# Rotary embedding and scores on one Trainium2 core: the first piece of q is issued on ScalarE's DMA queue instead of SyncE's

## The chip and the metric

The kernel runs on one core of one Trainium2 chip. The metric is the device time of one execution in microseconds. Engines are named as in the profile: PE is TensorE, PEld its weight loads, DVE is VectorE, ACT ScalarE, POOL GpSimd, SP SyncE.

## The reference

Queries and keys of 16 batches, 512 positions, 16 heads and 64 channels are rotated by the tables cos and sin, and then every query position of a head is multiplied with every key position of the same head. All is in float32.

```python
# q, k: (16, 512, 16, 64); cos, sin: (512, 32); q1, q2 (k1, k2) are the halves of the 64 channels
q_rot = concat([q1 * cos - q2 * sin, q1 * sin + q2 * cos])
k_rot = concat([k1 * cos - k2 * sin, k1 * sin + k2 * cos])
scores = einsum('bshd,bthd->bsht', q_rot, k_rot)      # (16, 512, 16, 512)
```

The inputs are 67 MB, the output is 268 MB.

## The kernel before

A batch is 512 positions. Partition p holds the positions 4p to 4p+3 (`C` = 4), so a batch of q or k is one tile of 128 partitions by 4 x 1024 numbers, 2 MB, loaded by one DMA (`load`, L122, on SyncE's queue). Five of these later loads go through GpSimd's queue instead (`load_around`, L84 and L98).

The work goes in 64 steps `i`, four for each batch; a step makes the scores of one of the four position groups, 128 positions by 16 heads by 512 keys, 4 MB. For a step, VectorE rotates (`rope`: products at L149 and L150, the sum at L154), TensorE transposes the rotated tiles into PSUM banks (L170), ScalarE or VectorE copies these to `qT_t` and `kT_t` (L185), TensorE multiplies (`scores`, L201), ScalarE copies the products to the staging tile `st` (L208), and SyncE issues the store: for the first batch one 1 MB store for each quarter of the heads (L211), later one 4 MB store for each step (L188). There are three staging buffers. The whole order is written out by hand (`tc.manual_schedule()`): on each engine instructions run in the order of the program, and a DMA is issued when its engine comes to it.

The first batch is treated otherwise, so that work can begin before 4 MB have come. Its q and k go into one tile, `early`, in pieces by heads: first four heads of k (`G` = 4 heads, 512 KB, 128 partitions x 4 runs of 1 KB), then four heads of q, then the other twelve heads of k (1.5 MB, runs of 3 KB), then those of q, each one DMA of `load_units` (L67). The two small tables `cos_t` and `sin_t` (64 KB each) are loaded on ScalarE's queue (L225). After its two loads ScalarE loads its function table, waits for `sin_t`, and makes `ss_t`, the sine with both signs (L232, L233). VectorE begins with the four heads of k, goes on with the four heads of q, and then, in the loop over `i` = 0 to 3, with the other head groups of the first batch and the first tiles of the second.

The order of the first issues on SyncE is: k four heads, q four heads, k twelve heads, q twelve heads, k of batch 1, q of batch 1 (L67 four times, L122 twice); next on SyncE come the stores of step 0.

Of the kernel before, what the change touches and what calls it, by code (L numbers as in the profile page):

```python
# [10 lines left out]
def kernel(  # L11
# [8 lines left out]
    nc = tc.nc  # L20
# [4 lines left out]
    B, S, H, D = q.shape  # L25
# [5 lines left out]
    G = H // C  # L31
# [27 lines left out]
    units = {}  # L59
    used = [0]  # L60

    def load_units(which, head, heads):
        n = C * heads * D
        t = early[:, used[0] : used[0] + n].rearrange("p (c e) -> p c e", c=C)
        used[0] += n
        src = dram[which][0, :, :, head : head + heads, :]
        nc.sync.dma_start(t.rearrange("p c (h d) -> p c h d", d=D), src)  # L67
        for h in range(0, heads, G):
            units[which, (head + h) // G] = t[:, :, D * h : D * (h + G)]

# [42 lines left out]
    def load(which, b):  # L113

        if b >= B:
            return
        t = in_pool.tile([P, C, H * D], fp32, tag=which + "_in", name=which + "_sb")
        batches[which, b] = t
        if (which, b) in RELIEVED:
            load_around(which, b, t)  # L120
        else:
            nc.sync.dma_start(t.rearrange("p c (h d) -> p c h d", h=H), dram[which][b])  # L122

    def rope(which, n):


        part = part_pool.tile([P, H * D], fp32, tag="part", name="part")
        if n < C:
            x = units[which, n]
            sv, k1, k2 = "p c (g j) -> p c g j", {"j": HD}, {"j": D}  # L130
            cs = cos_t.unsqueeze(2).to_broadcast((P, C, 2 * G, HD))
            ss = ss_v.unsqueeze(2).to_broadcast((P, C, G, D))
            pv = part.rearrange("p (c g j) -> p c g j", c=C, j=D)
            x5 = x.rearrange("p c (h x j) -> p c h x j", x=2, j=HD)
            p5 = part.rearrange("p (c h x j) -> p c h x j", c=C, x=2, j=HD)
            adds = [(x5[:, :, :, y], p5[:, :, :, 1 - y]) for y in range(2)]
        else:
            x = batches[which, n // C][:, n % C]
            sv, k1, k2 = "p (g j) -> p g j", {"j": HD}, {"j": D}
            cs = cos_t[:, n % C].unsqueeze(1).to_broadcast((P, 2 * H, HD))  # L140
            ss = ss_v[:, n % C].unsqueeze(1).to_broadcast((P, H, D))
            pv = part.rearrange(sv, **k2)
            x4 = x.rearrange("p (h x j) -> p h x j", x=2, j=HD)
            swapped = bass.AP(part.tensor, part.offset + HD, [part.ap[0], (D, H), (-HD, 2), (1, HD)])
            adds = [(x4, swapped)]
        xs, xc = x.rearrange(sv, **k2), x.rearrange(sv, **k1)

        def products():
            nc.vector.tensor_tensor(pv, xs, ss, op=mult)  # L149
            nc.vector.tensor_tensor(xc, xc, cs, op=mult)  # L150

        def sums():
            for y, z in adds:
                nc.vector.tensor_tensor(y, y, z, op=add)  # L154

        return [products, sums]
# [33 lines left out]
    def scores(i, p, st):  # L190

        ps = ps_s_pool.tile([P, 2, S], fp32, tag="ps_s", name="ps")
        b = i // C
        if b == 0:
            c, hp = divmod(p, 2)
            lhs, rhs = qT[i][:, C * hp + c], kT[0][:, 2 * i + hp]
        else:
            lhs, rhs = qT[i][:, p], kT[b][:, p]
        for r in range(2):
            po, rh = ps[:, r, :], rhs[64 * r : 64 * r + 64, :]  # L200
            nc.tensor.matmul(  # L201
                out=po, lhsT=lhs[64 * r : 64 * r + 64, :], rhs=rh, start=True, stop=True
            )
        so, si = st[:, 2 * p : 2 * p + 2, :], ps
        if b > 0:
            so = so.rearrange("s r (t c) -> s r t c", c=C)
            si = si.rearrange("s r (c t) -> s r t c", c=C)
        nc.scalar.copy(out=so, in_=si)  # L208
        if b == 0 and p % 2 == 1:
            c = p // 2  # L210
            nc.sync.dma_start(o_v[0, c, :, G * i : G * (i + 1)], st[:, G * c : G * (c + 1)])  # L211
        elif b > 0 and p == HP - 1:
            store(i, st)

    def tr_act(which, n):
        for g in range(2):
            transposed(which, n, g, nc.scalar.copy)

    def run(ops):
        for op in ops:  # L220
            op()

    with tc.manual_schedule():
        for t, src in ((cos_t, cos), (sin_t, sin)):
            nc.scalar.dma_start(t, src.rearrange("(p c) j -> p c j", c=C))  # L225
        for head, heads in ((0, G), (G, H - G)):
            load_units("k", head, heads)
            load_units("q", head, heads)
        load("k", 1)
        load("q", 1)  # L230
        make_identity(nc, ident)
        nc.scalar.copy(out=ss_t[:, :, 0, :], in_=sin_t)  # L232
        nc.scalar.mul(ss_t[:, :, 1, :], sin_t, -1.0)  # L233
        for which in ("k", "q"):
            run(rope(which, 0))
            tr_act(which, 0)


        for i in range(C):
            st = st_first[i] if i < 2 else stage_pool.tile([P, H, S], fp32, tag="stage", name="st")  # L240
            if i < C - 1:
                dve = rope("k", i + 1) + rope("q", i + 1) + rope("k", C + i)
                nxt = [("k", i + 1), ("q", i + 1)]
            else:
                dve = rope("q", C) + rope("k", C + i) + rope("q", C + 1) + rope("k", 2 * C)
                nxt = [("q", C), ("k", C + i)]
            for p in range(HP):
                scores(i, p, st)
                if p in (0, 1) and i > 0:
                    run(dve[:1])  # L250
                    dve = dve[1:]
                    transposed("k", C + i - 1, p, nc.vector.tensor_copy)
                if p == 3 and i < 2:
                    load("kq"[i], 2)
                if p in (2, 6):
                    m = len(dve) - (4 if p == 2 else 2) - (2 if i == C - 1 else 0)
                    run(dve[:m])
                    dve = dve[m:]
                    tr_act(*nxt.pop(0))
            run(dve)  # L260
        load("k", 3)


        for i in range(C, NST):
            tr = {}
            if i + 1 < NST:
                tr[1], tr[3] = ("q", i + 1, 0), ("q", i + 1, 1)
            if i + C < NST:
                tr[5], tr[6] = ("k", i + C, 0), ("k", i + C, 1)
            dve = []  # L270
            if i + 2 < NST:
                dve += rope("q", i + 2)
            if i + 1 + C < NST:
                dve += rope("k", i + 1 + C)
            st = stage_pool.tile([P, H, S], fp32, tag="stage", name="st")
            for p in range(HP):
                scores(i, p, st)
                if p not in tr:
                    continue
                if tr[p][0] == "q":  # L280
                    run(dve[:1])
                    dve = dve[1:]
                    transposed(*tr[p], nc.vector.tensor_copy)
                else:
                    transposed(*tr[p], nc.scalar.copy)
            run(dve)
            if i % C == C - 2:
                load("q", i // C + 2)
            elif i % C == C - 1:
                load("k", i // C + 3)  # L290
# [30 lines left out]
```

## Time and profile before

| what | value |
|---|---|
| runs | 793.13, 792.9, 793.66 us; median 793.13 us |
| span of the profiled execution, first to last instruction | 790.4 us |
| median of the runs less that span | 2.7 us |
| PE, ACT, DVE busy | 684.4, 562.0, 544.7 us |
| DMA | 336.18 MB, mean 425 GB/s over the span |
| first issue, first VectorE product, first store issued | 0.74, 5.67, 19.52 us |
| granted TensorE clock, mean | 0.934 |

The profile gives the span of its execution and not a time as the runs have it; the sum of the prediction is made against the span, and the 2.7 us outside it are added. Times in the profile count from the first instruction. A line "L67" is a line of the kernel before; in the changed kernel the lines of the last part lie one further down. A DMA is listed with its size and the time from its issue to its landing; a queue with its packets, MB and the time of its packets as a share of the 16 transfer engines' time (a share can be a little over 1, since packets overlap).

### The profile page before, as it was taken

The page shows a single profiled execution, that of the slowest core. Times are in us where ns is not written, and L with a number is a line of the kernel's source. Part 1 is how long each engine was busy: PE and PEld are TensorE (multiplying, and loading weights), DVE is VectorE, ACT ScalarE, POOL GpSimd, SP SyncE. Part 2 cuts the span into 40 slices and gives each one's busy share as a digit, 9 for nine tenths or more (in the row PEclk, how much of TensorE's full clock was granted, in tenths as well). Part 3 has the DMA queues.
Part 4 walks back from the last instruction along what each step waited for, and adds up shares of the span by engine and source line. Part 5 has one row for each costly group of instructions (what it writes and reads, how often), then busy time and mean ns, then how long its engine had stood idle before and what let it go on. Part 6 is the DMA issues. An engine that isn't in the chain of part 4 may idle for free.

```text
span 790.4 us, 7750 instructions
## 1 busy us (share of the span) xinstructions
PE 684.4 (87%) x3072; PEld 296.4 (38%) x3072; DVE 544.7 (69%) x516; ACT 562.0 (71%) x647; POOL 11.9 (2%) x24
## 2 busy tenths in 40 slices
PE   4989998988988889798996989889899798799960
PEld 2444443433433334343342433334334343344420
DVE  6999988666766678576785767667678487587400
ACT  3888886865857768486785866777577586588770
POOL 0000000000001000000000001000000000000000
PEclk9999999998999999898998989999899899899995
DMA  9999999999999999999999999999999999999997
GB/s 357 417 425 439 429 430 435 425 435 436 429 429 428 413 432 419 433 423 438 433 427 436 426 432 429 422 432 424 430 432 427 436 429 432 430 432 434 432 429 340
DMA packets 18836, 336.18 MB, mean 425 GB/s; under 512 B 2312, under 2 KB 3592, under 8 KB 4616
## 3 DMA queue, kind: packets, MB, share of 16 engines
q1 hardware_dynamic: 16704, 325.46, 96.4%
q0 software_dynamic: 1808, 10.10, 3.1%
q8 instruction: 24, 0.39, 0.2%
q10 hardware_dynamic: 288, 0.13, 0.1%
q14 instruction: 12, 0.10, 0.0%
HBM read 67.24 MB, written 268.44 MB: 425 GB/s over the span
## 4 chain that ended last, share of the span: by engine, by line
DMA 49%; PE 40%; ACT 5%; DVE 3%; issue 1%; ACTq 0%; SPq 0%; DVEq 0%
DMA out_dram<-st 46%; PE ps L201 30%; PE bank L170 10%; ACT st L208 5%; DMA q_sb<-in_q_dram 2%; DVE part L149 1%; DMA early<-in_k_dram 1%; DVE q_sb L150 0%; DVE k_sb L154 0%; DVE k_sb L150 0%; DVE q_sb L154 0%; DVE early L150 0%; DVE kT_t L185 0%; ACTq L316 0%; DVE early L154 0%
## 5 line engine op out<-in xcount | busy, mean ns | idle before, releaser
L208 ACT COPY st<-ps 128x1024 f32<-128x1024 f32 x512 | 495.7, 1020 | 192.6 <-DMA out_dram<-st 109.8
L201 PE MATMUL ps<-kT_t,qT_t 64*128 64x512 f32 x2048 | 544.0, 649 | 67.0 <-ACT st L208 67.0
L201 PEld LDWEIGHTS ps<-kT_t,qT_t 64*128 64x128 f32 x2048 | 183.6, 196 | 256.2 <-issue 133.3
L185 DVE COPY qT_t<-bank 128x512 f32<-128x512 f32 x118 | 81.6, 691 | 193.9 <-PE bank L170 193.9
L170 PEld LDWEIGHTS bank<-ident,q_sb 128*128 128x128 f32 x480 | 54.2, 149 | 99.0 <-issue 96.4
L170 PEld LDWEIGHTS bank<-ident,k_sb 128*128 128x128 f32 x480 | 50.3, 140 | 96.4 <-DVE k_sb L150 39.5
L170 PE MATMUL bank<-ident,q_sb 128*128 128x128 f32 x480 | 85.1, 304 | 0.9 <-PE ps L201 0.9
L170 PE MATMUL bank<-ident,k_sb 128*128 128x128 f32 x480 | 78.5, 286 | 1.6 <-DVE qT_t L185 1.2
L185 ACT COPY kT_t<-bank 128x512 f32<-128x512 f32 x122 | 72.4, 598 | 6.4 <-PE bank L170 6.4
L154 DVE TENSOR_TENSOR k_sb<-k_sb,part 128x1024 f32<-128x1024 f32 x60 | 73.5, 1225 | 2.1
L150 DVE TENSOR_TENSOR q_sb<-q_sb,cos_t 128x1024 f32<-128x1024 f32 x60 | 73.5, 1225 | 2.1
L150 DVE TENSOR_TENSOR k_sb<-k_sb,cos_t 128x1024 f32<-128x1024 f32 x60 | 73.5, 1225 | 2.0
L149 DVE TENSOR_TENSOR part<-q_sb,ss_t 128x1024 f32<-128x1024 f32 x60 | 73.5, 1225 | 2.0
L149 DVE TENSOR_TENSOR part<-k_sb,ss_t 128x1024 f32<-128x1024 f32 x60 | 73.0, 1216 | 0.9 <-DMA k_sb<-in_k_dram 0.7
L154 DVE TENSOR_TENSOR q_sb<-q_sb,part 128x1024 f32<-128x1024 f32 x60 | 72.9, 1216 | 0.0
L170 PE MATMUL bank<-ident,early 128*128 128x128 f32 x64 | 10.5, 315 | 12.4 <-DVE early L154 10.5
L170 PEld LDWEIGHTS bank<-ident,early 128*128 128x128 f32 x64 | 8.3, 161 | 17.4 <-issue 13.4
L149 DVE TENSOR_TENSOR part<-early,ss_t 128x1024 f32<-128x1024 f32 x8 | 9.8, 1222 | 5.8 <-DMA early<-in_k_dram 5.7
L98 POOL DMA_DIRECT2D q_sb<-in_q_dram x3 | 2.3, 752 | 620.2 <-PE bank L170 446.2
L154 DVE TENSOR_TENSOR early<-early,part 128x512 f32<-128x512 f32 x16 | 10.3, 687 | 0.2
L150 DVE TENSOR_TENSOR early<-early,cos_t 128x1024 f32<-128x1024 f32 x8 | 9.8, 1225 | 0.3
L185 ACT COPY qT_t<-bank 128x512 f32<-128x512 f32 x10 | 5.7, 629 | 3.2 <-PE bank L170 3.2
(12 smaller groups left out, 15.9 us busy)
## 6 DMA issues: line engine op xcount, KB each, us to landing
out_dram<-st SPq DMA_DIRECT2D x60, 4096.0 KB, 24.7
k_sb<-in_k_dram SPq DMA_DIRECT2D x13, 2048.0 KB, 28.3
q_sb<-in_q_dram SPq DMA_DIRECT2D x12, 2048.0 KB, 26.5
out_dram<-st SPq DMA_DIRECT2D x16, 1024.0 KB, 13.8
q_sb<-in_q_dram POOLq DMA_DIRECT2D x3, 1920.0 KB, 27.8
k_sb<-in_k_dram POOLq DMA_DIRECT2D x2, 1920.0 KB, 43.3
early<-in_k_dram SPq DMA_DIRECT2D x1, 1536.0 KB
early<-in_q_dram SPq DMA_DIRECT2D x1, 1536.0 KB
```

What stands on the lines that cost most here:

```text
L98: nc.gpsimd.dma_start(dst, src)
L149: nc.vector.tensor_tensor(pv, xs, ss, op=mult)
L150: nc.vector.tensor_tensor(xc, xc, cs, op=mult)
L154: nc.vector.tensor_tensor(y, y, z, op=add)
L170: nc.tensor.transpose(bank[:, x, :], src, ident)
L185: copy(out=dst, in_=src)
L201: nc.tensor.matmul(out=po, lhsT=lhs[64 * r : 64 * r + 64, :], rhs=rh, start=True, stop=True)
L208: nc.scalar.copy(out=so, in_=si)
```

## The change

`load_units` takes the engine that issues as an argument. The four heads of q are issued by ScalarE, after the two tables, and no longer by SyncE between the two pieces of k. The other three pieces and the loads of batch 1 stay on SyncE in their order. All sizes, destinations and waits stay as they are; in the compiled program one DMA issue leaves SyncE's list and one enters ScalarE's, ahead of the load of the function table.

```diff
-    def load_units(which, head, heads):
+    def load_units(which, head, heads, queue):
 ...
-        nc.sync.dma_start(t.rearrange("p c (h d) -> p c h d", d=D), src)
+        queue.dma_start(t.rearrange("p c (h d) -> p c h d", d=D), src)
 ...
         for t, src in ((cos_t, cos), (sin_t, sin)):
             nc.scalar.dma_start(t, src.rearrange("(p c) j -> p c j", c=C))
-        for head, heads in ((0, G), (G, H - G)):
-            load_units("k", head, heads)
-            load_units("q", head, heads)
+        load_units("k", 0, G, nc.sync)
+        load_units("q", 0, G, nc.scalar)
+        load_units("k", G, H - G, nc.sync)
+        load_units("q", G, H - G, nc.sync)
         load("k", 1)
         load("q", 1)
```

## The prediction

> **What bounds the kernel now.** I read the page's slices and queue table first, then a table of stretches, then the opening in order of time, then the DMA issues with their time to landing.
>
> The page (busy tenths of the DMA engines in 40 slices, and the queues; q1 is SyncE's, q0 GpSimd's, q10 ScalarE's, whose 0.13 MB are the two tables):
>
> ```profile
> DMA  9999999999999999999999999999999999999997
> ...
> q1 hardware_dynamic: 16704, 325.46, 96.4%
> q0 software_dynamic: 1808, 10.10, 3.1%
> ...
> HBM read 67.24 MB, written 268.44 MB: 425 GB/s over the span
> ```
>
> By stretches (last two columns: DMA share, GB/s):
>
> ```profile
> 2.00:4.00 2.00, 0.00 (x0) 0.00 (x0) 0.00 (x0) 0.91 (x1) 0.39 (x1) 1.00 0.74 207
> 4.00:6.00 2.00, 0.00 (x0) 0.00 (x0) 0.33 (x1) 0.51 (x2) 0.00 (x0) 1.00 1.09 374
> 6.00:9.00 3.00, 0.00 (x0) 0.00 (x0) 2.93 (x4) 0.00 (x0) 0.00 (x0) 1.00 1.00 371
> 9.00:13.00 4.00, 1.94 (x8) 1.57 (x8) 3.90 (x5) 1.17 (x2) 0.00 (x0) 1.00 1.03 416
> 20.00:100.00 80.00, 76.66 (x381) 35.13 (x381) 76.81 (x76) 67.12 (x82) 0.00 (x0) 1.00 1.01 428
> 783.00:788.99 5.99, 0.00 (x0) 0.00 (x0) 0.00 (x0) 0.00 (x0) 0.00 (x0) 0.50 0.51 219
> ```
>
> The 16 DMA engines are full from 4 us to about 783 us; only the ramp (2 to 4 us, share 0.74) and the last 6 us, in which the engines finish one after another, are not. So the time is: when the transfers start, plus the bytes at the going rate, plus that tail. A later instruction matters only if it lets the queue run dry.
>
> The opening in order of time (start, duration, engine, line):
>
> ```profile
> 0.74 0.66 SPq L67 DMA_DIRECT2D early<-in_k_dram  x1
> ...
> 1.46 0.60 SPq L67 DMA_DIRECT2D early<-in_q_dram  x1
> 1.63 1.28 ACT L232 ACT_TABLE_LOAD   x1 [1.63 <-PEq L305]
> ...
> 4.92 0.30 ACT L232 COPY ss_t<-sin_t 128x128 f32<-128x128 f32 x1 [2.00 <-DMA sin_t<-in_sin_dram]
> ...
> 5.67 1.23 DVE L149 TENSOR_TENSOR part<-early,ss_t 128x1024 f32<-128x1024 f32 x1 [5.67 <-DMA early<-in_k_dram]
> ...
> 9.52 1.23 DVE L149 TENSOR_TENSOR part<-early,ss_t 128x1024 f32<-128x1024 f32 x1
> ...
> 19.52 3.28 SPq L211 DMA_DIRECT2D out_dram<-st  x2
> ```
>
> The first piece of k (512 KB, landed 0.74 + 4.8 = 5.6 us) starts VectorE, which then works without a wait to about 67 us. The piece in question, q's first, lands at 1.46 + 5.6 = 7.1 us and is not touched before 9.52 us: 2.4 us early. SyncE is idle from 4.85 us to the first store at 19.52 us.
>
> How far the stores are from starving the queue (the second 1 MB store, issued at 22.46 us; the first 4 MB store, issued at 73.69 us; last number: us from issue to landing):
>
> ```profile
> out_dram<-st SPq DMA_DIRECT2D x1, 1024.0 KB, 7.3
> ```
> ```profile
> out_dram<-st SPq DMA_DIRECT2D x1, 4096.0 KB, 16.0
> ```
>
> At 425 GB/s these need 1.05 MB / 425 = 2.5 us and 4.19 / 425 = 9.9 us. The overhead of one transfer is at least 1.4 us (first k piece: issued at 0.74, first packets of q1 at about 2.2 us) and at most 4.8 - 1.2 = 3.6 us (its whole landing less 0.52 MB / 425). So the second store stood in the queue behind loads for 1.2 to 3.4 us and the 4 MB store for 2.5 to 4.7 us. Compute at the opening can be that much later before one transfer engine has nothing to do. Later stores land in 24.7 us (median), so the slack only grows.
>
> **The change part by part.** *SyncE loses one issue* of 0.60 us. The rest of k, the rest of q and batch 1 are issued 0.65 us earlier; nothing waits for SyncE then, and the packets stand behind the first k piece anyway. Worth zero.
>
> *ScalarE gains one issue* of about 0.6 us, at 1.6 us, ahead of its table load (1.63 to 2.91, then 2.2 to 3.5 us). The load is covered by the wait for the sine table until 4.92 us; were that cover gone it would cost 0.6 us on the two 0.30 us operations, which end at 5.4 us, still ahead of the k piece. No wait is added on any engine; the DVE instructions that read the piece wait for its own semaphore as before.
>
> *The 512 KB move from q1 to q10*, behind the sine table, and there compete with what is on q1. How two queues share: in 236 to 244 us a GpSimd load (8 KB packets) runs beside q1 (mostly 32 KB packets):
>
> ```profile
> q1 hardware_dynamic: 86, 2.79, 81.1%
> q0 software_dynamic: 86, 0.65, 19.1%
> ```
>
> They take turns packet by packet, whatever the size. The k and q first pieces are 512 packets of 1 KB each, the rest of k 512 packets of 3 KB. The sine packets on q10 thin out at about 4.25 us (51 records of q10 in 4.0 to 4.5 us, 14 in 4.25 to 5.5); by then q1 has moved 419 records, so some 95 packets of k's first piece are left. 1 KB packets go at 463 / 1.25 us = 370 per us (4.25 to 5.5 us), 3 KB ones at 271 / 2.25 us = 120 per us (6.75 to 9 us). With turns one to one: 95 pairs take 190 / 370 = 0.5 us instead of 0.26, so k's piece lands 0.25 us later (5.8 us). The remaining 417 packets of q alternate with 3 KB packets: 417 x (1/370 + 1/120) = 4.6 us, the last at 4.25 + 0.5 + 4.6 = 9.4 us, landed 0.4 to 1 us after that (the gaps of the two first pieces now): 9.8 to 10.4 us. VectorE wants it at 9.52 + 0.25 = 9.77 us. So VectorE, and the first store with it, comes 0.25 to 0.9 us later; I take 0.5 us. The rest of k has the same bytes ahead of it as now (landing near 10.9 us, used at 13.37 us). 0.5 us is below the smallest slack of 1.2 us: hidden, cost zero. If that cover were gone it would cost 0.5 us.
>
> *The transfers themselves.* Same packets, same engines, only another order; at the start either nothing or a gain. A gain is bounded by the ramp and the small packets: (1 - 0.74) x 2 = 0.5 us in 2 to 4 us, and 5 us at 372 instead of 416 GB/s, 0.55 us; together 1.05 us. A loss from switching queues is not seen: 429 GB/s in 236 to 244 us against 425 over the span. The k piece is still first on q1, so the start does not move; I take zero.
>
> [...]
>
> Sum: 0 us on the path. The profiled execution spans 790.4 us and the runs' median is 793.13 us, so 2.7 us lie outside the span and are not touched. Forecast 793.1 us.
>
> **The rivals.**
>
> *Slower: the piece is starved on q10.* For it: while the sine table was on q10, q1 moved 360 records in 3.0 to 4.5 us and q10 143, that is 2.5 to 1. Against it: a sine table is only 128 packets and q10 was empty at times. At 2.5 to 1 the 417 packets would wait for over 1000 packets of 3 KB, that is for all of k's and q's rest, and land where the rest of q lands now, about 14.7 us (q1's 4 MB at the rates above). VectorE is then 14.7 - 9.5 = 5.2 us late, the first stores as well, and with 1.2 to 2.4 us of slack the queue is dry for 2.8 to 4.0 us that never come back: 796 to 797 us. It decides from a landing of about 9.5 + 1.2 = 10.7 us on, and passes 0.2% from about 12.3 us on.
>
> *Faster: two queues fill the ramp.* For it: share 0.74 in 2 to 4 us, and 371 GB/s against 416 up to 9 us. Against it: q10 holds the sine table until about 4.3 us, so the new piece can't help in the ramp. In full it gives 1.05 us: 792.1 us, within 0.2%. To pass that, the tail has to shrink too: engines that finish late (0.49 x 6 us = 2.9 us idle in the last stretch) because they fell behind at the start; then 791 us.
>
> *Nothing happens at the transfers*: that q lands as before, before 9.5 us. Same time as the forecast.
>
> **How the numbers follow.** 0.2% is 1.6 us, about what a measurement of this kernel can tell from no change. Hidden, with up to 1 us either way from the ramp and the first stores: 0.66, of which the one with no shift at all is a third. Slower by starvation: 0.20, since the 2.5 to 1 row can't be dismissed and my slack has a low end of 1.2 us. Faster by over 0.2%: 0.14. The range goes from 793.1 less the 1.05 us, rounded down for the spread of the runs (0.4 us), 791.7 us, up into the starved case, to 795.6 us.
>
> **What would show it.** Right: the second VectorE L149 starts between 9.5 and 10.5 us, the first store at 19.5 to 20.5 us, DMA share 1.0 from 4 to 783 us, the second 1 MB store still lands over 5 us after its issue. Wrong: q's piece lands after 12 us, the 40 slices show a dip near 25 us, and the span grows by as much; or the GB/s before 9 us rise above 400 and the span shrinks.

## The result, and the profile after

The changed kernel takes 795.71 us (median of 8 runs, 794.36 to 796.75) where the kernel before takes 793.26 us (8 runs, 792.78 to 793.84). The ratio is 1.0029 with a 95% interval of 1.0019 to 1.0039: 2.3 us slower, 1.5 to 3.1 us. The forecast was 793.1 us and no measurable change; its range ended at 795.6 us.

The opening of the changed kernel in order of time (lines lie one further down from L229 on):

```profile
1.65 0.62 ACTq L67 DMA_DIRECT2D early<-in_q_dram  x1
...
2.30 1.28 ACT L233 ACT_TABLE_LOAD   x1 [2.30 <-issue]
...
5.13 0.30 ACT L233 COPY ss_t<-sin_t 128x128 f32<-128x128 f32 x1 [1.55 <-DMA sin_t<-in_sin_dram]
...
5.67 1.23 DVE L149 TENSOR_TENSOR part<-early,ss_t 128x1024 f32<-128x1024 f32 x1 [5.67 <-ACT ss_t L234]
...
12.34 1.23 DVE L149 TENSOR_TENSOR part<-early,ss_t 128x1024 f32<-128x1024 f32 x1 [2.86 <-DMA early<-in_q_dram]
...
22.70 0.35 SPq L211 DMA_DIRECT2D out_dram<-st  x1
```

VectorE starts at the same moment as before (5.67 us), but its second block starts at 12.34 instead of 9.52 us, after 2.86 us of waiting for q's piece. The first store follows 3.18 us later than before. The issues of the opening with their time to landing:

```profile
early<-in_k_dram SPq DMA_DIRECT2D x1, 512.0 KB, 4.2
early<-in_q_dram ACTq DMA_DIRECT2D x1, 512.0 KB, 10.6
```

So q's piece landed at 1.65 + 10.6 = 12.25 us instead of 7.1 us. k's first piece came 4.2 us after its issue instead of 4.8, but that can't be put down to the change: another execution of the changed kernel has 5.0 us, and the runs with q's piece left on SyncE have 4.4 to 4.8 us.

By stretches (last two columns: DMA share and GB/s):

```profile
2.00:4.00 2.00, 0.00 (x0) 0.00 (x0) 0.00 (x0) 1.28 (x1) 0.39 (x1) 1.00 0.85 228
4.00:6.00 2.00, 0.00 (x0) 0.00 (x0) 0.33 (x1) 0.51 (x2) 0.00 (x0) 1.00 1.01 366
6.00:9.00 3.00, 0.00 (x0) 0.00 (x0) 2.93 (x4) 0.00 (x0) 0.00 (x0) 1.00 1.04 395
9.00:13.00 4.00, 1.94 (x8) 1.57 (x8) 1.14 (x2) 1.17 (x2) 0.00 (x0) 1.00 1.04 408
24.00:40.00 16.00, 16.00 (x86) 7.74 (x84) 15.14 (x16) 14.66 (x20) 0.00 (x0) 1.00 0.98 360
```

Up to 24 us the transfers are not slower than before; from 2 to 24 us they run at 395 GB/s, before at 392. The loss lies between 24 and 40 us. The same stretch of the kernel before, in the same columns:

```profile
24.00:40.00 16.00, 16.00 (x86) 7.82 (x86) 15.50 (x17) 12.68 (x17) 0.00 (x0) 1.00 1.01 424
```

(424 - 360) / 424 x 16 us = 2.4 us of transfers are missing there, about the whole difference of the runs. From 40 to 760 us both kernels move 430 GB/s. The spans of the two profiled executions differ by more (793.8 - 790.4 = 3.4 us): the changed kernel's profiled run took 795.59 us, 1.8 us outside its span, while 2.7 us separate the median of before from its span, so the profiled execution of before was probably a quick one. The comparison of runs is what counts.

### The profile page after: what moved, and what is told of

Same layout as the page of the kernel before. It is cut to its first block, busy times and chain, and to the rows that moved or that the text cites. A ratio compares the mean times of both kernels' runs of the same rounds, so it can differ in the third digit from the quotient of the medians.

```text
span 793.8 us, 7750 instructions
## 1 busy us (share of the span) xinstructions
PE 684.9 (86%) x3072; PEld 297.1 (37%) x3072; DVE 544.5 (69%) x516; ACT 561.8 (71%) x647; POOL 12.0 (2%) x24
## 4 chain that ended last, share of the span: by engine, by line
DMA 46%; PE 40%; DVE 5%; ACT 5%; issue 1%; ACTq 0%; DVEq 0%
DMA out_dram<-st 45%; PE ps L201 30%; PE bank L170 10%; ACT st L208 5%; DVE part L149 2%; DMA early<-in_q_dram 1%; DVE early L154 1%; DVE k_sb L154 1%; DVE k_sb L150 1%; DVE early L150 1%; DVE kT_t L185 0%; DVE q_sb L150 0%; DVE q_sb L154 0%; ACTq L317 0%; ACTq L225 0%
## 5 line engine op out<-in xcount | busy, mean ns | idle before, releaser
L170 PE MATMUL bank<-ident,q_sb 128*128 128x128 f32 x480 | 86.7, 308 | 0.9 <-PE ps L201 0.9
```

The costliest lines, as they stand in the source:

```text
L170: nc.tensor.transpose(bank[:, x, :], src, ident)
```

## The experiments

**The theory, and its rival.** Theory: q's piece lands late, VectorE and with it all stores are late, and SyncE's queue has too little work meanwhile. Rival: the transfers themselves suffer from having two queues. All runs were timed in five rounds beside the kernel before, except the second profile of the changed kernel, which is one execution; differences in us are the ratio to the kernel before, less one, times 793.3 us. First stores and GB/s come from one profiled execution of each kernel.

**Lateness alone, in three sizes.** Extra products in the kernel before, on data that is there, with no DMA touched:

```diff
         for which in ("k", "q"):
+            if which == "q":
+                spin(1)     # 2, 3: so many products part <- early(k), ss_t of 1.22 us
             run(rope(which, 0))
             tr_act(which, 0)
```

> The kernel before with one extra VectorE product (1.22 us, on data that is there, its result unused) ahead of the work on q's first piece; no DMA is changed. Lateness theory (q's piece lands late, the first stores follow, SyncE's queue runs out of work): first store at about 20.7 us, within the slack, so 0 to +0.6 us. Rival, the transfers themselves suffer from having two queues: no change, as for any such delay.

> The kernel before with two extra VectorE products (2.45 us) ahead of the work on q's first piece; no DMA is changed. Lateness theory: first store at about 22.0 us, +0.6 to +2.0 us. Rival (two queues as such): no change.

> The kernel before with three extra VectorE products (3.7 us) ahead of the work on q's first piece; no DMA is changed. Lateness theory: first store at about 23.2 us, a little later than in the changed kernel (22.70 us), so +2.4 to +3.5 us, and the loss shows as fewer GB/s between 24 and 40 us. Rival (two queues as such): no change.

| extra products | added to VectorE | first store (profile) | GB/s, 24 to 40 us | time against before |
|---|---|---|---|---|
| 0 | 0 | 19.52 us | 424 | |
| 1 | 1.2 us | 20.96 us | 408 | 1.0011 [1.0003, 1.0020]: +0.9 us [0.2, 1.6] |
| 2 | 2.4 us | 21.39 us | 393 | 1.0026 [1.0018, 1.0034]: +2.1 us [1.4, 2.7] |
| 3 | 3.7 us | 22.89 us | 360 | 1.0041 [1.0028, 1.0054]: +3.3 us [2.2, 4.3] |
| changed kernel | 2.86 us wait | 22.70 us | 360 | 1.0029 [1.0019, 1.0039]: +2.3 us [1.5, 3.1] |

With one, two and three extra products, 24 to 40 us:

```profile
24.00:40.00 16.00, 16.00 (x86) 7.75 (x84) 15.65 (x16) 14.10 (x18) 0.00 (x0) 1.00 1.01 408
24.00:40.00 16.00, 15.86 (x85) 7.51 (x82) 15.66 (x17) 14.50 (x19) 0.00 (x0) 1.00 1.00 393
24.00:40.00 16.00, 16.00 (x84) 7.65 (x82) 15.66 (x18) 14.70 (x20) 0.00 (x0) 1.00 0.98 360
```

A delay of VectorE by itself makes the same loss in the same place. The rival asked for no change in all three. The loss is also larger than the theory expected: 1.2 us of lateness should have cost 0 to 0.6 us, and each microsecond costs about 0.9. The profiled execution with two products was the quickest of its twelve (793.52 us), so its first store and GB/s may show too little.

**The change with the lateness taken back.**

```diff
-            run(rope(which, 0))
+            run(rope(which, 0) if which == "k" else [])
             tr_act(which, 0)
```

> The changed kernel without the rotation of q's first piece (four heads of the first batch are left unrotated), which takes 3.8 us off VectorE just where q's piece comes late; all DMAs as in the changed kernel. Lateness theory: the first store is at 18 to 20 us again and the time is that of the kernel before, within 0.4 us. Rival (two queues as such): still 2.4 us slower than before.

First store at 18.90 us, ratio 0.9989 [0.9980, 0.9997], 0.9 us below before [0.2, 1.6], and between 24 and 40 us:

```profile
24.00:40.00 16.00, 16.00 (x84) 7.45 (x82) 14.52 (x17) 12.06 (x16) 0.00 (x0) 1.00 1.01 426
```

The two queues and ScalarE's issue are all there, and nothing of the loss is. The rival, which asked for 2.4 us, has fallen. This run leaves out work, so why it is even a little quicker than before stays open; the kernel with the cosine table on SyncE, below, shows the same without leaving anything out.

**More work in the queue.** If the queue only lacks work for a moment, an earlier load should cover it:

```diff
         load("q", 1)
+        load("k", 2)
 ...
-                if p == 3 and i < 2:
-                    load("kq"[i], 2)
+                if p == 3 and i == 1:
+                    load("q", 2)
```

> The changed kernel with the load of k of batch 2 (2 MB) issued right behind the loads of batch 1 at the start, and no longer behind two stores of step 0; its buffer is free from the beginning. q's first piece lands as late as in the changed kernel (about 12.2 us) and the first store is as late (about 22.7 us), but SyncE's queue holds 2.1 MB / 425 GB/s = 4.9 us more of work. Lateness theory: the late store is hidden, the GB/s between 24 and 40 us are back at 420 or more, and the time is that of the kernel before or up to 1 us below. Rival (two queues as such, or ScalarE's part of the change): still about 2.4 us slower than before.

This expectation failed: 1.0024 [1.0015, 1.0033], 1.9 us slower than before [1.2, 2.6]. Its profile says where:

```profile
24.00:40.00 16.00, 16.00 (x84) 7.52 (x80) 15.69 (x16) 14.70 (x19) 0.00 (x0) 1.00 1.00 421
100.00:120.00 20.00, 20.00 (x99) 8.82 (x98) 17.09 (x16) 17.34 (x21) 0.00 (x0) 1.00 1.00 389
```

The loss between 24 and 40 us is gone (421 GB/s), but a new one stands at 100 to 120 us: 389 GB/s where the kernel before has 435 there, (435 - 389) / 435 x 20 us = 2.1 us. The first 4 MB store, issued at 76.26 us, shows the narrow place:

```profile
out_dram<-st SPq DMA_DIRECT2D x1, 4096.0 KB, 13.2
```

13.2 us from issue to landing, of which 9.9 us are its own transfer at 425 GB/s; before it was 16.0 us, in the changed kernel 15.5 us. After q's piece VectorE waits for no DMA up to 120 us, and it pauses for TensorE no longer than before (4.0 us in the changed kernel, 4.4 us before), so the lateness stays in every store of that time: in the changed kernel the first 4 MB store is issued at 76.87 us, 3.18 us later than before, like the first store of all. So there are two narrow places in the queue, and the kernel with three extra products shows both (360 GB/s in 24 to 40 us, 410 in 100 to 120 us). My reading, which no run tests by itself, is that work moved ahead of the first place is missing at the second.

The same early load without q's move, and with both loads of batch 2 early:

> The kernel before with the same early load of k of batch 2. Lateness theory: the cover is not needed or only a little, 0 to -1 us, and the same time as the changed kernel with the early load. If the early load costs something by itself (stores land 4.9 us later, ScalarE waits longer for a staging buffer), it shows here as a plus.

> The kernel before with both loads of batch 2 (4 MB) issued at the start. Lateness theory: as with k alone, 0 to -1 us; or slower, if the stores that now stand 9.8 us further back hold up ScalarE at the staging buffers for so long that the queue runs dry later.

With k alone 0.9996 [0.9987, 1.0004]: no difference. With k and q 1.0037 [1.0023, 1.0052], 2.9 us slower: ScalarE waits 7.2 us for a staging buffer where it waited 2.6 us before, the first 4 MB store lands 12.7 us after its issue, and 394 GB/s are left between 100 and 120 us. That fits its second expectation: with still more work ahead of them the stores hold their buffers longer, and what waits for a buffer is late again.

**Why q's piece was late: its start.** The cosine table goes to SyncE, behind the first piece of k, so that q's piece is issued earlier and the rest of k later:

```diff
-        for t, src in ((cos_t, cos), (sin_t, sin)):
-            nc.scalar.dma_start(t, src.rearrange("(p c) j -> p c j", c=C))
+        nc.scalar.dma_start(sin_t, sin.rearrange("(p c) j -> p c j", c=C))
         load_units("k", 0, G, nc.sync)
         load_units("q", 0, G, nc.scalar)
+        nc.sync.dma_start(cos_t, cos.rearrange("(p c) j -> p c j", c=C))
```

> The changed kernel with the cosine table issued on SyncE behind the first piece of k, so that q's piece is issued on ScalarE behind the sine table alone, at about 1.15 us, and the rest of k later, at about 1.8 us. If the transfers of both queues are made ready in the order of issue, one after another, q's first packets come ahead of those of the rest of k (by about 4.5 us) and the piece lands at 9 to 10 us: time within 0.8 us of before. If a transfer on ScalarE's queue has a long lead of its own (3.9 us from issue to first packet in the changed kernel), the first packets come at 5 us or later, the piece lands at about 11.5 us, and the time is 1.5 to 2.4 us above before.

First the changed kernel: queue records in 4.75 to 5.5 us, then in 5.5 to 6.5 us (packets, MB, share):

```profile
q1 hardware_dynamic: 91, 0.28, 99.0%
```
```profile
q1 hardware_dynamic: 105, 0.32, 93.7%
q10 hardware_dynamic: 22, 0.02, 6.3%
```

The sine table had ended by 4.75 us; q10 then stays empty until after 5.5 us and has only 22 packets by 6.5 us, though q's piece was issued at 1.65 us (by the packet records its first one starts at 5.64 us, and the first of the rest of k at 4.25 us). The packets of the rest of k (3 KB: 0.28 MB in 91 packets), issued 0.2 us earlier on the other engine, come first. Now the kernel with the cosine table on SyncE, 4 to 4.5 us and 4.75 to 5.5 us:

```profile
q10 hardware_dynamic: 138, 0.14, 85.3%
q1 hardware_dynamic: 53, 0.04, 23.5%
```
```profile
q10 hardware_dynamic: 174, 0.18, 77.7%
q1 hardware_dynamic: 97, 0.04, 23.1%
```

q's piece (issued at 1.18 us) flows by 4.25 us, and q1 has only the cosine table's 512 B packets (0.04 MB in 97) beside it, issued at 1.46 us; the rest of k, issued at 2.10 us, comes later. In both kernels transfers of the two queues begin in the order in which they were issued, not each as soon as its own queue is free.

```profile
early<-in_q_dram ACTq DMA_DIRECT2D x1, 512.0 KB, 5.6
```

The piece lands 5.6 us after its issue, at 6.8 us (sooner than the 9 to 10 us expected), the first store is issued at 18.66 us, and the time is that of before: 0.9996 [0.9987, 1.0005]. So q's piece on ScalarE's queue does no harm; its place behind other transfers does.

Which transfers count, the packet records suggest but do not settle. Four times a transfer has the same number of packets issued ahead of it on both engines together, 1280: the rest of k in the kernel before, q's piece in the changed kernel, the rest of k in this one, and q's piece in the next. Their first packets start at 5.60, 5.64, 5.63 and 5.69 us, although on their own queues 1024, 256, 640 and 256 packets are ahead. (In other profiles with the changed kernel's order q's piece starts as late as 6.2 us.) That speaks for one order over both queues. But each of the four is also the third transfer of its own queue, and no run here separates the two.

**Why it was late: the turns.** The rest of k in three pieces, with packets of 1 KB as q's:

```diff
-        load_units("k", G, H - G, nc.sync)
+        for head in range(G, H, G):
+            load_units("k", head, G, nc.sync)
```

> The changed kernel with the rest of k (twelve heads) loaded by three DMAs of four heads instead of one, so that all its packets have 1 KB as q's; the first third is still issued ahead of q's piece. If q's piece is late for two reasons, its late start (first packets at about 5.5 us) and taking turns with packets three times its size, the second is gone: 512 pairs of 1 KB packets take 512 x 2 / 370 = 2.8 us instead of 6 us, the piece lands at 8.5 to 9.5 us, VectorE does not wait for it, and the time is within 0.8 us of before. If the late start alone counts, the piece still lands after 11.5 us and the time stays about 2.3 us above before.

The changed kernel between 7 and 11 us:

```profile
q1 hardware_dynamic: 413, 1.22, 75.3%
q10 hardware_dynamic: 410, 0.42, 29.4%
```

413 to 410: one packet each, though one kind is three times the other's size. With 1 KB packets on both sides the piece starts as late (after 5.5 us) but lands sooner:

```profile
early<-in_q_dram ACTq DMA_DIRECT2D x1, 512.0 KB, 7.9
```

That is at 1.65 + 7.9 = 9.55 us; VectorE's second block starts at 10.01 us without waiting for it, the first store is issued at 20.12 us. So both count for the landing, the late start and the turns with larger packets: of the 5.2 us between 7.1 and 12.25 us about 2.5 us are there with equal packets too, from the late start and turns one to one, which alone uses up the 2.4 us to spare; the larger packets make the other 2.7 us. The time is 1.0013 [1.0004, 1.0023], +1.0 us [0.3, 1.8], a little over the 0.8 us expected. What is left of the loss is not a wait for q's piece: in this execution VectorE already began 0.5 us late (at 6.17 us, waiting for `ss_t`), and from 2 to 10 us the smaller packets move 318 GB/s where the kernel before has 336, (336 - 318) / 425 x 8 us = 0.3 us.

**Together, and once more.**

> The two edits that did no harm put together: q's piece on ScalarE behind the sine table alone, the cosine table on SyncE, and k of batch 2 loaded at the start. First store at about 18.7 us with 4.9 us more in the queue. If any starvation is left in the kernel before, this takes it away: 0 to -1 us against before.

0.9994 [0.9985, 1.0002]: not told apart from before. The first store came at 20.01 us and not at 18.7: VectorE's second block is 0.3 us later than with the cosine table alone (9.35 against 9.05 us), and the first twelve score products of TensorE take 4.64 us instead of 3.55. So the first store of a single profile can move by about 1 us without any wait for q's piece; it came at 18.66, 19.52 and 20.12 us with the cosine table on SyncE, in the kernel before and with the rest of k in three pieces, where the first twelve score products took 3.55, 3.99 and 4.10 us. No version here beats the kernel before by more than the measurement can tell, apart from the one that leaves out work.

> The changed kernel once more, unaltered, for a second look at the stretch from 24 to 40 us: if the loss there belongs to the late stores, the rate is again 345 to 380 GB/s and the first store again at 22 to 23 us; if it was a chance of the one execution, the rate is 410 or more.

The second profile has the same loss: 371 GB/s between 24 and 40 us, first store at 22.27 us, q's piece 10.9 us after its issue.

**What the loss looks like from inside.** Between 24 and 40 us of the changed kernel the queue runs short for a few tenths of a microsecond, once:

```profile
26.00:27.00 1.00, 1.00 (x6) 0.19 (x2) 0.97 (x2) 1.00 (x2) 0.00 (x0) 1.00 0.67 279
```

Over the whole stretch the share is 0.98, and yet less is moved. Queue records of the changed kernel in 32 to 35 us, while it loads k of batch 2, and of the kernel before during the same load, 29 to 32 us:

```profile
q1 hardware_dynamic: 52, 0.85, 101.2%
```
```profile
q1 hardware_dynamic: 83, 1.29, 100.2%
```

52 packets fill three microseconds of 16 engines where 83 did: 48 / 52 = 0.92 us for one on average instead of 0.58. The packet records of all five kernels of the table give the sum. Nearly every packet of the kernel before takes 0.31 us (8 KB, stores) or 0.61 us (16 KB, loads) between 24 and 40 us. What packets took beyond that, added up and divided by 16 engines, and the time for which engines had no packet in hand:

| extra products | packets took longer | engines without a packet |
|---|---|---|
| 0 | 0.1 us | 0.0 us |
| 1 | 0.8 us | 0.0 us |
| 2 | 1.2 us | 0.1 us |
| 3 | 2.1 us | 0.4 us |
| changed kernel | 2.1 us | 0.5 us |

So most of the loss is packets that take longer, and with one extra product all of it. The slow packets are not the load's alone: between 28 and 29 us of the changed kernel 40 store packets of 8 KB take 0.51 us on average. One run asked whether that load, beside the stores, is the cause:

```diff
-                if p == 3 and i < 2:
+                if (i, p) in ((0, 7), (1, 3)):
                     load("kq"[i], 2)
```

> The changed kernel with the load of k of batch 2 issued behind all four stores of step 0 instead of behind two. The stores stay late and the queue is as shallow or shallower. If the loss between 24 and 40 us is the lateness alone, it stays or grows: 360 GB/s or less, +2.3 us or more against before. If it is that load running beside stores in a shallow queue, the packets between 27 and 36 us are at full rate again and the loss falls to what a dry queue explains, under 1.2 us.

Most of the slow packets went with the load: 426 GB/s in 28 to 31 us, when four stores of step 0 are in hand, and 306 GB/s in 36.5 to 39.5 us, when the load runs. But the loss did not fall: 378 GB/s over 24 to 40 us, and 1.0034 [1.0022, 1.0046], +2.7 us [1.7, 3.7]. Neither expectation is met in full (360 GB/s or less for the one, under 1.2 us for the other), but the time speaks against the load beside stores as the cause. Where the loss shows moves with the load; that it comes depends on the late stores. Why packets take longer when the queue is short, though each engine has one in hand, is not settled by these runs.

## Why the prediction was wrong, point by point

- *What bounds the kernel.* The transfers, and the lost time is lost transfer time: this held (2.4 us of transfers missing between 24 and 40 us, 2.3 us of time).
- *SyncE's issue and ScalarE's table load at no cost*: held. VectorE starts at 5.67 us as before; `ss_t` is what it waits for last (ready at 5.64 us), as it is in four of the five profiles with q's piece left on SyncE and something else changed (with k of batch 2 loaded early the chain begins with the sine table, landed at 1.16 + 4.08 = 5.24 us), so that does not come from the move.
- *Turns one to one, whatever the size*: held for 3 KB against 1 KB (413 to 410). Nor are the turns long there: from 8 to 8.3 us the packet records of the changed kernel repeat every 0.16 us, and in each such time 16 packets of 3 KB and 16 of 1 KB start, as many of each as there are engines; one of each takes 0.12 + 0.05 us.
- *"The sine packets on q10 thin out at about 4.25 us", and q's follow*: this is the first step that failed. I took the end of the queue's own predecessor for the start of the piece. It began after 5.5 us, behind the rest of k that had been issued 0.2 us earlier on the other engine, so all of its 512 packets, not 417, took turns with 3 KB packets. With the measured start my own term comes out right: 5.6 + 512 x (1/370 + 1/120) = 11.3 us, landed 0.4 to 1 us later, 11.7 to 12.3 us. Landing 12.25 us instead of 9.8 to 10.4; lateness at the first store 3.2 us instead of 0.5. The k piece, forecast 0.25 us later, shows no such shift (4.2 and 5.0 us in the two profiles, 4.4 to 4.8 us with q's piece on SyncE).
- *"0.5 us is below the smallest slack of 1.2 us: hidden."* This is the second, and it is what turns the lateness into a loss. The waiting time of one store in the queue was read as a cover that is free until it is used up. As a measure of when an engine has nothing to do it was fair: with one extra product no engine was without a packet, with three and in the changed kernel for 0.4 to 0.5 us. But the three delays show that 1.2 us already costs 0.9 us (0.2 to 1.6), in packets that take longer. The table of stretches could not show that packets take longer before the queue runs dry, and I looked at the two narrow places one by one, not at how a lateness of VectorE goes through both. "Later stores land in 24.7 us, so the slack only grows" passed over what comes between them: the early load moved the loss to 100 to 120 us.
- *The rivals.* The slower one is what happened: a landing from 10.7 us on was to decide it, and it was 12.25 us. Its reason, turns of 2.5 to 1, was wrong, so it got the sign right partly by luck. By its own sum a lateness of 3.2 us less a slack of 1.2 to 2.4 us gives 0.8 to 2.0 us; 2.3 us [1.5, 3.1] were measured, and by the three delays there was no slack to take off.
- *A gain from filling the ramp* is at most small (228 against 207 GB/s in 2 to 4 us, 395 against 371 in 6 to 9 us; but over 2 to 24 us 395 against 392, (395 - 392) / 424 x 22 us = 0.16 us), and single profiles of kernels with q's piece left on SyncE differ by more (391 to 401 GB/s over 2 to 24 us).
- *"2.7 us lie outside the span."* In the runs, each with its time and its span on record, 1.7 to 1.9 us do. The sum set the span of one quick execution against a median of runs; the forecast itself is that median and is not touched.

## What to carry to other kernels

In these runs a transfer moved to another engine's queue did not start when that queue was free (q10 was empty from 4.67 us), but behind what had been issued before it (5.64 us), and it took turns by packets (410 of its own to 413 of the other queue). So look for what is issued just ahead of it on any engine, and at the packet sizes it will take turns with. A landing with 2.4 us to spare lost all of that by a late start beside equal packets (2.5 us), and as much again by a neighbour with packets three times its size (2.7 us). And a queue that stands full by the share of busy time is no proof that compute can be late (with one extra product the share was 1.01 between 24 and 40 us, and the time 0.9 us longer): delay an engine on purpose by two or three sizes and read the slope.

## What the runs showed of the hardware that was not expected

Transfers issued on SyncE's and ScalarE's queues began in the order of their issues across both queues: with 0.2 us between two issues, the later one's first packets came after 5.5 us, on an empty queue of its own, while the other's filled the engines from 4.75 us at the latest. Two queues took turns of one packet each, 3 KB against 1 KB (413 to 410 between 7 and 11 us). And transfers can be slow without the engines being idle: three microseconds of a 2 MB load ran at 284 GB/s with a share of 1.01 when its first packet came 3.4 us after its issue, and at 429 GB/s when it came 5.5 us after.
